# Slab weight sums of a Strassen-style down projection: the second row's sum made by an accumulating DMA, VectorE's two sums placed behind the second job

## The chip, the cores and the metric

The kernel runs on one core of one Trainium2 chip. A core has a matrix engine (TensorE, PE in the profile, with its weight loads listed apart as PEld), VectorE (DVE), ScalarE (ACT), GpSimd (POOL) and SyncE (SP), and 16 DMA engines that serve the queues of all of them. In this kernel SP issues the plain loads and POOL the loads that add to what is in place already (accumulating DMAs). The metric is the device time of one execution in microseconds.

## The reference

A two-layer decoder trunk in float32 on 256 tokens with width 2048. Each layer has a mixer and then a squared-ReLU MLP with 8192 hidden channels:

```python
def squared_relu_mlp(h, w1, w2):
    z = jax.nn.relu(h @ w1)
    return (z * z) @ w2
...
    x = x + jnp.concatenate([token_out, mem_out], axis=-1) @ w_out[i]
    x = x + squared_relu_mlp(rms_norm(x, ffn_norm[i]), w_ff1[i], w_ff2[i])
```

The mixers (causal pooling in the first layer, differential attention in the second, memory cross-attention in both) are not touched by the change. It concerns the product with `w_ff2` in both layers.

## The kernel before

All weights lie in DRAM as rows of 128 partitions x 1024 floats, in the order of their use. A weight that PE is to use is split in two: ScalarE casts it to PE's rounded format (the high part, line 178), and VectorE subtracts that from the weight (the low part, line 181). Both go to a ring of six slots of 512 columns. Each product is then three matmuls: low activations by high weights, high by high, and high by low (lines 867, 869, 870).

The feed (class `Feed`) does this ahead of PE. It holds a list of steps, `prep`, worked out by a dry run of the whole program (class `Plan`): N steps for 512 columns of an ordinary matrix, S steps for the jobs of a slab, and K steps for sums. When PE's program reaches a job, `fill` prepares up to six steps beyond it, as far as slots are free, and `load` issues DMAs up to three or four rows beyond what the step needs. SP issues ordinary rows (`raw`, line 135), a slab's first row (line 139), its second row (line 143) and the left half of a running sum (line 152).

Down projection by slabs. Most of `w_ff2` is multiplied by a scheme of the Strassen-Winograd kind: the 256 tokens are two halves, 256 rows of the weight are two blocks of 128, and 1024 columns are two halves of 512. A slab has four weight pieces: B11 and B21 in its first row in DRAM (`ra` in the code, left and right half), B12 and B22 in its second (`rb`). Instead of eight products it takes seven, on sums of pieces, in four jobs:

- job 0 uses B11 and B21, the untouched first row;
- job 1 uses the running sum `t1` = B11 + B12. It is made by DMA: SP loads B11, and POOL adds B12 to it with an accumulating DMA (line 153). There are three buffers for it, and it is fetched a slab ahead;
- job 2 uses the second row: in its left half t2 = t1 - B22, made by VectorE (line 204, the K step, ahead of job 0), and in its right half B22;
- job 3 uses the first row after VectorE has replaced it (line 218, 1024 columns, right behind the low part of job 0): t2 - B11 and t2 - B21.

The seven products are summed in seven PSUM banks (`banks`), two groups of columns by turns; sums of activations for them are made on VectorE (lines 792 to 795). At the end of each half the banks are put together with additions and subtractions (`close_left`, `finish_banks`). There are 60 slabs in each of the two layers. For even slabs both rows come from a pool of three buffers named `slab`; the second row of an odd slab lies in a fixed piece of the tile `room`, as do the running sums, so the profile names these `room`.

The order in which each engine gets its instructions is set by the framework's scheduler from the program's order and the dependences, and by a few hints (`order`) that put one instruction behind another. Up-projection tiles (`x_bank`, weights from `raw`) and slab jobs alternate by a table of due times (`tiles_at`). The program is symmetric in the two layers.

Of the kernel before, what the change touches and what calls it, by code (L numbers as in the profile page):

```python
# [17 lines left out]
P = 128  # L18
# [37 lines left out]
class Plan:  # L56
# [13 lines left out]
    def close(self):  # L70
        prep = []
        for job in self.jobs:

            if job[0] == "S" and job[2] == 0:
                prep.append(("K", job[1]))
            prep.append(job)
        self.prep = prep
        self.where = {job: i for i, job in enumerate(prep)}
        self.loads = []
        self.need = {}  # L80
        for p in prep:
            if p[0] == "K":
                self.loads += [("S", p[1], 0), ("S", p[1], 1)]
            elif p[0] == "N" and p[1] % 2 == 0:
                self.loads.append(("N", p[1] // 2))
            self.need[p] = len(self.loads) - 1
        rows = sorted(self.loads, key=lambda r: r[0] == "N" and 8 * r[1] + 8 > self.npos)
        self.row = {r: h for h, r in enumerate(rows)}
        of = {}
        pos = 0  # L90
        for what in self.entries:
            of.setdefault(pos // 8, []).append(what)
            pos += what[4]
        self.order = []
        for r in rows:
            self.order += of[r[1]] if r[0] == "N" else self.slabs[r[1]][r[2]]


class Feed:
# [22 lines left out]
    def load(self, upto):  # L122
        while self.lp < min(upto, len(self.plan.loads)):
            r = self.plan.loads[self.lp]
            h = self.plan.row[r]
            n = 1024
            if r[0] == "N":
                n = min(1024, (self.plan.npos - 8 * r[1]) * P)
                t = self.wpool.tile([P, 1024], F32, tag="raw", bufs=RAWS, name=f"raw{h}")
            elif r[2] and r[1] % 2:  # L130
                t = self.spare
            else:
                t = self.rows.tile([P, 1024], F32, tag="rows", bufs=3, name=f"slab{h}")
            if r[0] == "N":
                self.nc.sync.dma_start(t[:, 0:n], self.wst[h, :, 0:n])
            elif r[2] == 0:
                if r[1] % PER_PART == 0:
                    self.first_sum(r[1])
                self.nc.sync.dma_start(t, self.wst[h])
                if (r[1] + 1) % PER_PART:  # L140
                    self.first_sum(r[1] + 1)
            else:
                self.nc.sync.dma_start(t[:, 512:1024], self.wst[h, :, 512:1024])
            self.raw[r] = t
            self.lp += 1

# [41 lines left out]
        return True  # L188

    def _prepare(self, p):  # L190
        sub, add = self.nc.vector.tensor_sub, self.nc.vector.tensor_add
        self.load(self.plan.need[p] + 1 + self.loads_ahead)
        if p[0] == "N":
            r = ("N", p[1] // 2)
            c = p[1] % 2 * 512
            if not self._split(p, self.raw[r][:, c : c + 512], 1):
                return False
            if c:
                del self.raw[r]
            return True  # L200
        ra, rb = self.raw[("S", p[1], 0)], self.raw.get(("S", p[1], 1))
        t1 = self.t1[p[1] % len(self.t1)]
        if p[0] == "K":
            one = sub(rb[:, 0:512], t1, rb[:, 512:1024])
            if p[1] % PER_PART:
                self.order(one, self.last_low.ins.name)
            if self.gate:

                self.order(one, self.gate)
                self.gate = None  # L210
            return True
        src, n = ((ra, 2), (t1, 1), (rb, 2), (ra, 2))[p[2]]
        if not self._split(p, src, n):
            return False
        if p[2] == 0:
            t2 = rb[:, 0:512].unsqueeze(1).to_broadcast([P, 2, 512])
            two = ra.rearrange("p (a c) -> p a c", a=2)
            sub(two, t2, two)
        if p[2] == 1:
            self.t1_of[p[1] % len(self.t1)] = None  # L220
        if p[2] == 3:
            del self.raw[("S", p[1], 0)], self.raw[("S", p[1], 1)]
        return True

# [67 lines left out]
def program(ctx, tc, plan, dry, xT, memT, par, lam, cst, wst, yT):  # L292
# [437 lines left out]
    def ffn(l, xs, tags, done):  # L730
# [35 lines left out]
        def convert(j):  # L766
            a = stage[j % 8]
            k = j % NK

            def high():  # L770
                z_free[k] = False
                nc.scalar.copy(z[:, k, 0:T], a)
                at(1, low)

            def low():
                nc.vector.tensor_sub(z[:, k, T : 2 * T], a, z[:, k, 0:T].bitcast(F32))
                z_done.add(j)

            when(lambda: z_free[k], high)
            if j % 2 == 0:  # L780
                return
            i = j // 2

            def ready():
                return j in z_done and j - 1 in z_done and sit_free[i % 4]

            def combine():
                sit_free[i % 4] = False
                a11, a21 = stage[2 * i % 8][:, 0:P], stage[2 * i % 8][:, P:T]
                a12, a22 = stage[(2 * i + 1) % 8][:, 0:P], stage[(2 * i + 1) % 8][:, P:T]  # L790
                s1, s2, s3, s4 = (sums[i % 2][:, c * P : c * P + P] for c in range(4))
                nc.vector.tensor_add(s1, a21, a22)
                nc.vector.tensor_sub(s3, a11, a21)
                nc.vector.tensor_sub(s2, s1, a11)
                nc.vector.tensor_sub(s4, a12, s2)
                at(1, sums_high)
                at(2, sums_low)

            def sums_high():
                nc.scalar.copy(sit[i % 4][:, 0:512], sums[i % 2])  # L800

            def sums_low():
                nc.vector.tensor_sub(
                    sit[i % 4][:, 512:1024], sums[i % 2], sit[i % 4][:, 0:512].bitcast(F32)
                )
                sit_done.add(i)

            when(ready, combine)
# [63 lines left out]
        def slab_jobs(g, i, again, end):  # L872
            k = 2 * i
            first = 2 if g == 0 else 0
            n = feed.slab(
                [
                    [("w_ff2", l, k, c, 4), ("w_ff2", l, k + 1, c, 4)]
                    for c in (first, first + 1)
                ]
            )  # L880

            def plain(c, t):
                assert k + c in z_done
                zk = z[:, (k + c) % NK, :]
                return zk[:, t * P : t * P + P], zk[:, T + t * P : T + t * P + P]

            def summed(c):
                assert i in sit_done
                s = sit[i % 4]
                return s[:, c * P : c * P + P], s[:, 512 + c * P : 512 + c * P + P]  # L890

            sides = (
                ((0, lambda: plain(0, 0)), (1, lambda: plain(1, 0))),
                ((2, lambda: summed(0)),),
                ((3, lambda: summed(1)), (4, lambda: summed(3))),
                ((5, lambda: summed(2)), (6, lambda: plain(1, 1))),
            )

            def run(j):
                hi, lo = feed.job(n, j)  # L900
                for c, (p, a) in enumerate(sides[j]):
                    s = slice(512 * c, 512 * c + 512)
                    assert holds[p] == g
                    product(p, g, end, a(), hi[:, s], lo[:, s])
                feed.job_used(n, j)
                if j == 3 and not again:
                    sit_free[i % 4] = True
                    if i < 24:
                        z_free[k % NK] = z_free[(k + 1) % NK] = True

            return run
# [6 lines left out]
        holds = [0] * 7  # L918
        back = [False] * 7
        saved = {}  # L920
        of_job = ((0, 1), (2,), (3, 4), (5, 6))

        def restore(p, g):
            if (g, p) in saved:
# [16 lines left out]
        def close_left(j):  # L941
# [8 lines left out]
                nc.scalar.copy(left["v"], banks[2])  # L950
            elif j == 2:
                left["c12"] = keep.pop(0)
                add(left["u"], left["u"], banks[3])
                sub(left["c12"], left["v"], left["u"])
                add(left["c12"], left["c12"], banks[4])
            else:
                u, v = left["u"], left["v"]
                add(u, u, banks[5])
                sub(v, v, u)
                sub(u, u, banks[6])  # L960
            for p in of_job[j]:
                restore(p, 0)
            if j == 3:
# [27 lines left out]
        def finish_banks():  # L991
# [9 lines left out]
            add(c11, u, p2)  # L1001
            add(u, u, p6)
            sub(c12, v, u)
            add(u, u, p7)
            add(c12, c12, p3)
            sub(v, v, u)
            sub(u, u, p4)
            for c, t in ((c11, 0), (c12, 0), (u, 1), (v, 1)):
                scale_rows(c, t)

# [627 lines left out]
```

## Time and profile before

| what | value |
|---|---|
| median of 3 runs | 2010.63 us (2010.59 to 2010.78) |
| span of the profiled execution | 2010.7 us |
| PE busy | 1999.0 us (99%) |
| VectorE busy | 1779.2 us (88%) |
| ScalarE busy | 1525.3 us (76%) |
| POOL busy | 157.1 us (8%) |
| moved by DMA | 422.19 MB, 210 GB/s |
| accumulating DMAs | 120, each 256 KB |

The profiled execution's span is the kernel's time to within 0.1 us, with nothing around it. Busy times of matmuls are modelled at their ends, so a busy PE can still hide short waits; these stand in the view of waits. A DMA share is the time of packets over 16 engines, and can exceed 1 where packets wait on each other. L178 and the like are line numbers of the kernel before.

### The profile page before, as it was taken

The page shows a single profiled execution, that of the slowest core. Times are in us where ns is not written, and L with a number is a line of the kernel's source. Part 1 is how long each engine was busy: PE and PEld are TensorE (multiplying, and loading weights), DVE is VectorE, ACT ScalarE, POOL GpSimd, SP SyncE. Part 2 cuts the span into 40 slices and gives each one's busy share as a digit, 9 for nine tenths or more (in the row PEclk, how much of TensorE's full clock was granted, in tenths as well). Part 3 has the DMA queues.
Part 4 walks back from the last instruction along what each step waited for, and adds up shares of the span by engine and source line. Part 5 has one row for each costly group of instructions (what it writes and reads, how often), then busy time and mean ns, then how long its engine had stood idle before and what let it go on. Part 6 is the DMA issues. An engine that isn't in the chain of part 4 may idle for free.

```text
span 2010.7 us, 31966 instructions
## 1 busy us (share of the span) xinstructions
PE 1999.0 (99%) x10510; PEld 1696.5 (84%) x10510; DVE 1779.2 (88%) x3096; ACT 1525.3 (76%) x2838; POOL 157.1 (8%) x187
## 2 busy tenths in 40 slices
PE   9999999999999999999999999999999999999999
PEld 8888888888888888888888888888888888888877
DVE  8888888989999999999765698878989999999998
ACT  7765577787887888878665699557787878878885
POOL 0001310000000000100000000320000000100000
PEclk9999999999999999999999999999999999999999
DMA  8555576777778777755575533567777777777773
GB/s 319 171 188 195 188 221 208 232 221 229 226 226 240 223 218 234 225 175 175 181 235 194 178 127 126 199 197 229 224 214 233 225 234 223 231 230 231 223 228 124
DMA packets 145030, 422.19 MB, mean 210 GB/s; under 512 B 16352, under 2 KB 19040, under 8 KB 144864
## 3 DMA queue, kind: packets, MB, share of 16 engines
q1 hardware_dynamic: 127440, 388.69, 57.5%
q0 software_dynamic: 17280, 31.46, 9.7%
q8 instruction: 82, 1.34, 0.3%
q14 instruction: 84, 0.69, 0.1%
q10 hardware_dynamic: 144, 0.01, 0.0%
HBM read 418.00 MB, written 2.10 MB: 209 GB/s over the span
## 4 chain that ended last, share of the span: by engine, by line
PE 93%; ACT 3%; DVE 2%; issue 1%; DMA 0%; ACTq 0%; DVEq 0%
PE x_bank L433 21%; PE x_bank L435 11%; PE p L867 9%; PE p L870 9%; PE p L869 9%; PE wo L433 6%; PE wo L435 3%; PE u L433 2%; ACT hi_ring L178 1%; PE ff L433 1%; PE u L435 1%; PE k L469 1%; PE q L467 1%; PE q L469 1%; PE q L468 1%; PE v L468 1%
## 5 line engine op out<-in xcount | busy, mean ns | idle before, releaser
L178 ACT CAST hi_ring<-raw 128x512 fp32r<-128x512 f32 x969 | 593.5, 623 | 267.3 <-PE x_bank L433 61.1
L181 DVE TENSOR_TENSOR lo_ring<-raw,hi_ring 128x512 fp32r<-128x512 f32 x969 | 662.0, 695 | 105.1 <-ACT hi_ring L178 93.5
L433 PE MATMUL x_bank<-fx,hi_ring 128*128 128x512 f32 x1952 | 610.8, 394 | 0.0
L435 PEld LDWEIGHTS x_bank<-fx,lo_ring 128*128 128x128 f32 x1952 | 365.1, 188 | 88.1 <-DVE lo_ring L181 6.1
L181 DVE TENSOR_TENSOR lo_ring<-slab,hi_ring 128x1024 fp32r<-128x1024 f32 x300 | 366.4, 1221 | 50.1 <-ACT hi_ring L178 48.8
L178 ACT CAST hi_ring<-slab 128x1024 fp32r<-128x1024 f32 x300 | 314.6, 1053 | 117.2 <-PE p L869 65.0
L435 PE MATMUL x_bank<-fx,lo_ring 128*128 128x256 f32 x1952 | 384.8, 278 | 1.5 <-DVE lo_ring L181 1.5
L433 PEld LDWEIGHTS x_bank<-fx,hi_ring 128*128 128x128 f32 x1952 | 320.7, 189 | 26.8 <-ACT room L761 1.3
L153 POOL DMA_DIRECT2D room<-in_w x120 | 104.0, 872 | 1139.7 <-DMA room<-in_w 1121.4
L867 PE MATMUL p<-hi_ring,sit 128*128 128x512 f32 x480 | 190.5, 397 | 0.4 <-ACT hi_ring L178 0.2
L869 PE MATMUL p<-hi_ring,sit 128*128 128x512 f32 x480 | 187.9, 391 | 0.0
L870 PE MATMUL p<-lo_ring,sit 128*128 128x512 f32 x480 | 186.5, 391 | 0.2
L433 PE MATMUL wo<-cat,hi_ring 128*128 128x512 f32 x512 | 161.8, 397 | 0.3 <-DVE rc L404 0.3
L181 DVE TENSOR_TENSOR lo_ring<-room,hi_ring 128x512 fp32r<-128x512 f32 x180 | 154.3, 863 | 5.7 <-ACT hi_ring L178 5.6
L178 ACT CAST hi_ring<-room 128x512 fp32r<-128x512 f32 x180 | 138.1, 769 | 19.0 <-PE p L869 9.5
L867 PE MATMUL p<-hi_ring,z 128*128 128x512 f32 x360 | 141.2, 392 | 0.7 <-ACT hi_ring L178 0.7
L869 PE MATMUL p<-hi_ring,z 128*128 128x512 f32 x360 | 140.6, 391 | 0.0
L870 PE MATMUL p<-lo_ring,z 128*128 128x512 f32 x360 | 139.7, 392 | 0.0
L435 PEld LDWEIGHTS wo<-cat,lo_ring 128*128 128x128 f32 x512 | 95.9, 188 | 22.0
L870 PEld LDWEIGHTS p<-lo_ring,sit 128*128 128x128 f32 x480 | 89.8, 188 | 21.8 <-DVE lo_ring L181 2.7
L867 PEld LDWEIGHTS p<-hi_ring,sit 128*128 128x128 f32 x480 | 90.0, 187 | 15.6 <-ACT hi_ring L178 5.8
L435 PE MATMUL wo<-cat,lo_ring 128*128 128x256 f32 x512 | 101.5, 279 | 0.0
(370 smaller groups left out, 3339.9 us busy)
## 6 DMA issues: line engine op xcount, KB each, us to landing
raw<-in_w SPq DMA_DIRECT2D x484, 512.0 KB, 4.3
slab<-in_w SPq DMA_DIRECT2D x120, 512.0 KB, 4.4
room<-in_w SPq DMA_DIRECT2D x180, 256.0 KB, 3.3
room<-in_w POOLq DMA_DIRECT2D x120, 256.0 KB, 5.7
slab<-in_w SPq DMA_DIRECT2D x60, 256.0 KB, 4.3
memraw<-in_mem SPq DMA_DIRECT2D x5, 512.0 KB, 4.5
resid<-in_x SPq DMA_DIRECT2D x8, 256.0 KB, 5.5
out_y<-resid SPq DMA_DIRECT2D x16, 128.0 KB, 1.9
```

Of the source, the lines that this page charges most:

```text
L153: self.nc.gpsimd.dma_start(self.t1[i], right, accum_op=ALU.add)
L178: self.last_cast = self.nc.scalar.copy(hi, src)
L181: low = self.nc.vector.tensor_sub(lo, src, hi.bitcast(F32))
L433: nc.tensor.matmul(ps, hi, xs[:, k, :], start=first and c == 0, stop=False)
L435: nc.tensor.matmul(ps[:, T : 2 * T], lo, xs[:, k, 0:T], start=False, stop=last and c == len(ks) - 1,)
L467: nc.tensor.matmul(ps[t], x[t][1], hi, start=k == 0, stop=False)
L468: nc.tensor.matmul(ps[t], x[t][0], hi, start=False, stop=False)
L469: nc.tensor.matmul(ps[t], x[t][0], lo, start=False, stop=k == NK - 1)
L867: nc.tensor.matmul(ps, a[1], hi, start=new, stop=False, **again)
L869: nc.tensor.matmul(ps, a[0], hi, start=False, stop=False, **again)
L870: nc.tensor.matmul(ps, a[0], lo, start=False, stop=end, **again)
```

## The change

- The second row is loaded whole, 512 KB instead of its right half of 256 KB, and POOL then adds B22 to its left half with a second accumulating DMA. That half becomes B12 + B22, where it was t2 = B11 + B12 - B22.
- VectorE's two sums per slab become plain additions of 512 columns on the first row: its left half becomes t1 + B22, and its right half that plus B21. The sum of 1024 columns goes.
- These two stand in the K step, which moves from ahead of job 0 to behind job 1, and a hint puts the first of them behind the low part of job 1.
- The scheme of seven products is another one of the same family. So signs change in the sums of activations and in the closing of the banks, and the products with sums 1 and 2 change places: job 2 now holds banks 5 and 4, and job 3 banks 3 and 6.

```diff
@@ class Plan, close
-            if job[0] == "S" and job[2] == 0:
+            prep.append(job)
+            if job[0] == "S" and job[2] == 1:
                 prep.append(("K", job[1]))
-            prep.append(job)
...
-            if p[0] == "K":
+            if p[0] == "S" and p[2] == 0:
                 self.loads += [("S", p[1], 0), ("S", p[1], 1)]
@@ class Feed, load
-                self.nc.sync.dma_start(t[:, 512:1024], self.wst[h, :, 512:1024])
+                self.nc.sync.dma_start(t, self.wst[h])
+                self.nc.gpsimd.dma_start(t[:, 0:512], self.wst[h, :, 512:1024], accum_op=ALU.add)
@@ class Feed, _prepare
         if p[0] == "K":
-            one = sub(rb[:, 0:512], t1, rb[:, 512:1024])
-            if p[1] % PER_PART:
-                self.order(one, self.last_low.ins.name)
+            one = add(ra[:, 0:512], t1, rb[:, 512:1024])
+            self.order(one, self.last_low.ins.name)
+            add(ra[:, 512:1024], ra[:, 0:512], ra[:, 512:1024])
...
-        if p[2] == 0:
-            t2 = rb[:, 0:512].unsqueeze(1).to_broadcast([P, 2, 512])
-            two = ra.rearrange("p (a c) -> p a c", a=2)
-            sub(two, t2, two)
-        if p[2] == 1:
+        if p[2] == 3:
             self.t1_of[p[1] % len(self.t1)] = None
-        if p[2] == 3:
@@ ffn, combine
-                nc.vector.tensor_add(s1, a21, a22)
-                nc.vector.tensor_sub(s3, a11, a21)
+                nc.vector.tensor_sub(s1, a21, a22)
+                nc.vector.tensor_sub(s3, a21, a11)
                 nc.vector.tensor_sub(s2, s1, a11)
-                nc.vector.tensor_sub(s4, a12, s2)
+                nc.vector.tensor_add(s4, a12, s2)
@@ ffn, slab_jobs
-                ((3, lambda: summed(1)), (4, lambda: summed(3))),
-                ((5, lambda: summed(2)), (6, lambda: plain(1, 1))),
+                ((5, lambda: summed(2)), (4, lambda: summed(3))),
+                ((3, lambda: summed(1)), (6, lambda: plain(1, 1))),
...
-        of_job = ((0, 1), (2,), (3, 4), (5, 6))
+        of_job = ((0, 1), (2,), (5, 4), (3, 6))
@@ ffn, close_left
-                add(left["u"], left["u"], banks[3])
-                sub(left["c12"], left["v"], left["u"])
-                add(left["c12"], left["c12"], banks[4])
+                add(left["c12"], left["v"], banks[4])
+                sub(left["c12"], left["c12"], left["u"])
+                sub(left["u"], left["u"], banks[5])
...
-                add(u, u, banks[5])
+                sub(left["c12"], left["c12"], banks[3])
+                add(u, u, banks[3])
                 sub(v, v, u)
-                sub(u, u, banks[6])
+                add(u, u, banks[6])
@@ ffn, finish_banks
-            add(u, u, p7)
+            sub(u, u, p7)
...
-            sub(u, u, p4)
+            add(u, u, p4)
```

More of the change, by code (lines that the diff above doesn't have):

```diff
@@ L190, in _prepare @@
     def _prepare(self, p):
-        sub, add = self.nc.vector.tensor_sub, self.nc.vector.tensor_add
+        add = self.nc.vector.tensor_add
         self.load(self.plan.need[p] + 1 + self.loads_ahead)
```

## The prediction

> **What bounds the kernel now.** I read the page's busy table and chain first, to find the engine that sets the end.
>
> ```profile
> PE 1999.0 (99%) x10510; PEld 1696.5 (84%) x10510; DVE 1779.2 (88%) x3096; ACT 1525.3 (76%) x2838; POOL 157.1 (8%) x187
> PE 93%; ACT 3%; DVE 2%; issue 1%; DMA 0%; ACTq 0%; DVEq 0%
> ```
>
> PE is busy 1999.0 of 2010.7 us and makes up 93% of the chain; VectorE is second. The change does not touch the number of matmuls, so it can only win what PE waits for, and can lose as much as late weights cost. Slabs exist only in the two squared-ReLU layers, so I then cut those into stages, with two dense moments beside them.
>
> ```profile
> core 0: us, PE busy (x) PEld busy (x) DVE busy (x) ACT busy (x) POOL busy (x), PEclk, DMA share, GB/s
> 10.00:15.00 5.00, 5.00 (x24) 4.14 (x23) 4.72 (x15) 5.00 (x12) 0.00 (x0) 1.00 1.03 410
> 400.00:600.00 200.00, 199.70 (x1019) 168.66 (x1018) 184.43 (x275) 163.33 (x281) 16.44 (x19) 1.00 0.74 225
> 600.00:800.00 200.00, 199.83 (x1018) 168.78 (x1017) 188.31 (x281) 167.28 (x281) 17.30 (x20) 1.00 0.77 230
> 1400.00:1600.00 200.00, 199.55 (x1022) 168.88 (x1022) 182.42 (x273) 160.06 (x273) 16.42 (x19) 1.00 0.74 224
> 1600.00:1800.00 200.00, 199.99 (x1018) 169.17 (x1017) 190.01 (x284) 162.45 (x271) 16.67 (x20) 1.00 0.76 229
> 1589.00:1594.00 5.00, 5.00 (x27) 4.26 (x26) 5.00 (x7) 4.71 (x10) 0.86 (x1) 1.00 1.04 346
> ```
>
> In the slab stages VectorE is busy 92 to 95%, and the DMA engines show a share of 0.74 to 0.77. The POOL column counts the accumulating DMAs: 19 or 20 in 200 us, so one slab takes about 10.3 us. The waits of PE and of its weight loads then say what a lighter VectorE can give back.
>
> ```profile
> PEld x_bank L435 <- DVE lo_ring L181: 7.8, 21, 1.0
> PEld p L867 <- ACT hi_ring L178: 7.3, 23, 0.5
> PEld p L870 <- DVE lo_ring L181: 5.3, 18, 0.5
> PE x_bank L435 <- DVE lo_ring L181: 2.0, 5, 0.6
> ```
>
> Columns: waiter, releaser, us in total, times, longest. VectorE ends 7.8 + 5.3 + 2.0 = 15.1 us of waits. That is the ceiling of the gain; weight loads run beside matmuls, so the part seen in the time is smaller.
>
> **Term 1, VectorE.** Per slab one 512-wide and one 1024-wide sum go, and two 512-wide additions come.
>
> ```profile
> L204 DVE TENSOR_TENSOR slab<-room,slab 128x512 f32<-128x512 f32 x60 | 41.1, 685 | 10.6 <-DMA room<-in_w 10.6
> L218 DVE TENSOR_TENSOR slab<-slab,slab 128x1024 f32<-128x1024 f32 x60 | 73.1, 1218 | 0.0
> ```
>
> Each has a twin of 60 for the other slabs. Saved per slab: 0.685 + 1.218 - 2 x 0.685 = 0.53 us, times 120 = 64 us of VectorE, 5% of a 10.3 us slab, so its share there falls from about 93 to 88%. Swapping additions and subtractions in the activations' sums and in the bank sums has the same shapes and costs nothing; the closing of the left half has one 512-wide operation more, 0.7 us per layer, on an engine that then has over 10% free. Gain on the path: between 0 (PE's waits stay, since other casts set them) and 15.1 us. I take a quarter, 3.8 us: of the rows above, the weight-load ones are partly hidden, and the waits at the layers' ends have other causes too.
>
> The 10.6 us in the first row are VectorE's waits for the first slab's running sum, once per layer; the new place of the sums, behind job 1, which needs that sum anyhow, makes them disappear from VectorE. I count no time for it: PE is fed from slots filled earlier.
>
> Where the two sums now stand, seen on VectorE for one odd slab in the first layer (slab_4509 before, slab_4526 after, is its first row; room holds its second row and the running sum). Before:
>
> ```order
> L204 TENSOR_TENSOR room_2604<-room_2604 128x512
> L181 TENSOR_TENSOR lo_ring<-slab_4509,hi_ring 128x1024
> L181 TENSOR_TENSOR lo_ring<-room_2604,hi_ring 128x512
> L218 TENSOR_TENSOR slab_4509<-room_2604,slab_4509 128x1024
> L181 TENSOR_TENSOR lo_ring<-raw_4499,hi_ring 128x512
> ```
>
> and after:
>
> ```order
> L182 TENSOR_TENSOR lo_ring<-slab_4526,hi_ring 128x1024
> L182 TENSOR_TENSOR lo_ring<-room_2604,hi_ring 128x512
> L205 TENSOR_TENSOR slab_4526<-room_2604 128x512
> L182 TENSOR_TENSOR lo_ring<-raw_4516,hi_ring 128x512
> L207 TENSOR_TENSOR slab_4526<-slab_4526 128x512
> ```
>
> The first sum moved behind the low parts of jobs 0 and 1, and the second is half as wide.
>
> **Term 2, the second accumulating DMA.** It stands in POOL's queue, which runs in order. Before, POOL held only the running sums between the squares of two layers:
>
> ```order
> L706 TENSOR_TENSOR psq<-resid 128x256
> L707 TENSOR_TENSOR acc<-acc,psq 128x256
> L153 DMA room_2604<-in_w 128x512 x60
> L700 TENSOR_TENSOR acc<-resid 128x256
> L706 TENSOR_TENSOR psq<-resid 128x256
> ```
>
> and after, at the start of that run:
>
> ```order
> L154 DMA room_2604<-in_w 128x512 x3
> L144 DMA room_2604<-in_w 128x512
> L154 DMA room_2604<-in_w 128x512
> L144 DMA slab_3025<-in_w 128x512
> L154 DMA room_2604<-in_w 128x512
> ```
>
> Running sums (L154) and second-row sums (L144) alternate. The first operand of job 2 thus changes from a VectorE product to: load landed, then POOL issues, then the sum landed. Durations, and one of the tighter (even) slabs from load to use:
>
> ```profile
> L143 SPq DMA_DIRECT2D slab<-in_w x60: 327/328/328, 104.8 to 1959.0; - x60
> DMA to landing us min/median/max: 2.5/4.0/6.9
> L153 POOL DMA_DIRECT2D room<-in_w x120: 856/865/1226, 257.7 to 1954.3; - x120
> DMA to landing us min/median/max: 3.6/5.7/8.0
> 613.23 0.33 SPq L143 DMA_DIRECT2D slab<-in_w  x1
> 617.31 0.33 SPq L152 DMA_DIRECT2D room<-in_w  x1
> 619.38 0.33 SPq L143 DMA_DIRECT2D room<-in_w  x1
> 621.29 0.86 POOL L153 DMA_DIRECT2D room<-in_w  x1 [8.94 <-DMA room<-in_w]
> 626.09 1.05 ACT L178 CAST hi_ring<-slab 128x1024 fp32r<-128x1024 f32 x1
> 628.05 1.22 DVE L181 TENSOR_TENSOR lo_ring<-slab,hi_ring 128x1024 fp32r<-128x1024 f32 x1
> 630.90 1.05 ACT L178 CAST hi_ring<-slab 128x1024 fp32r<-128x1024 f32 x1 [0.84 <-PE x_bank L433]
> 630.93 0.40 PE L867 MATMUL p<-hi_ring,sit 128*128 128x512 f32 x1
> 636.39 1.05 ACT L178 CAST hi_ring<-room 128x1024 fp32r<-128x1024 f32 x1 [0.59 <-PE p L869]
> 644.99 0.62 ACT L178 CAST hi_ring<-room 128x512 fp32r<-128x512 f32 x1
> ```
>
> The second row is issued at 613.23 and job 2's cast starts at 626.09. The load lands after 4.0 us, the sum 5.7 us after POOL starts it: 613.23 + 4.0 + 0.1 + 5.7 = 623.0, so 3.1 us early. The low part ends at 629.27 and PE first uses the job at 630.93, which adds 1.7 us: the chain may grow by 4.8 us before PE feels it. The next, odd slab has more: its second row, issued at 619.38, is cast at 636.39, 17.0 us later instead of 12.9. Job 3, which reads VectorE's two sums, is cast only at 630.90, so their new place does not hold it up. POOL has the time: 2 x 0.87 us per 10.3 us. A running sum that queues behind a second-row sum loses at most some 4 us; the one loaded at 617.31 is cast two slabs later, at 644.99. SP issues as many DMAs as before; its running-sum load (L152) now waits for the moved sum too, about 1 us later, and delays what is queued behind it. That is the loads of the other weights, for which ScalarE hardly ever waits:
>
> ```profile
> ACT hi_ring L178 <- DMA raw<-in_w: 6.3, 4, 2.4
> ```
>
> so I count nothing; without that cover it would be up to 1 us per slab.
>
> **Term 3, DMA traffic.** Per slab the load grows by 256 KB (the left half) and the sum reads 256 KB more: 0.524 MB per 10.3 us, 51 GB/s. Two readings of what that means:
>
> ```profile
> q1 hardware_dynamic: 127440, 388.69, 57.5%
> q0 software_dynamic: 17280, 31.46, 9.7%
> slab<-in_w SPq DMA_DIRECT2D x120, 512.0 KB, 4.4
> ```
>
> By packets' time: q0 doubles (9.7% of 2010.7 = 195 us) and q1 grows by 31.46 MB x 1156 us / 388.69 MB = 94 us; 289 us over 120 slabs is 2.4 us per 10.3 us, a share of 0.23 on top of 0.74 to 0.77, so 0.97 to 1.00. By bytes: 225 to 230 GB/s become about 280, while the stage at 1589 to 1594, with running sums in the mix, moved 346 at a share of 1.04, so 333 at 1.00; that is 84%. Packets' time contains waiting for one another (the share exceeds 1 in both dense rows), so bytes are nearer to capacity, and I take 84%: the DMA engines are close to full but not the bound. The larger load costs little in landing: 512 KB landed in 4.4 us against 4.0 us. Price of late sums: 0 at least; at most the rivals below. I take 1.4 us, some five even slabs late by 0.3 us.
>
> The Trainium skill (DMA: Bandwidth & Descriptors, Latency and other measured facts) puts HBM access at 0.2 us on average and 2 us at high load. By that rule each of the two landings could grow by 1.8 us, an estimate from the page, and the sum would still hold since 3.6 us is under 4.8. The trace agrees in kind, with medians 1.5 and 2.1 us above the minima at a share of 0.75; it is why the second rival below is not given less.
>
> **Sum.** 2010.7 (the profiled span; the median of the runs, 2010.63, is the same) - 3.8 + 1.4 = 2008.3 us. About 0.2%, 4 us, is what I take as telling a change from none; so this is no change.
>
> **Rivals.**
> 1. VectorE's relief is worth more: half of the 15.1 us or more goes, and no sum is late: 2010.7 - 7.5 = 2003.2. For it: VectorE at 95% in the later stages. Against: 7.3 us of waits are ended by ScalarE, which has as much work as before.
> 2. Slower: the two landings of the second-row sum lengthen under the added traffic. Place: job 2's cast, with ScalarE's queue held behind it. It decides when both together grow by more than 4.8 us on even slabs; an average of 0.3 us late on 60 slabs is 18 us: 2010.7 - 2.4 + 18 = 2026. For it: landings already reach 6.9 and 8.0 us, 5.2 us above the medians together. Against: those are the extremes.
> 3. Slower: the DMA engines run out. If packets' time is the true measure and the second sums stretch other packets, the demand passes 1.00; 2% over, on 120 slabs of 10.3 us, is 25 us: 2036, with all weight loads late and not only the sums. It decides at a capacity below 280 GB/s for this mix.
>
> **Chances.** The forecast 0.45 (its own range 2006.7 to 2014.6), rival 1 0.20, rival 2 0.23, rival 3 0.12. So faster 0.20, same 0.45, slower 0.35. The range goes from 2002, under rival 1, to 2036, which leaves out the upper half of rival 3 and a little of each of the others.
>
> **What the new profile would show.** VectorE's busy time near 1715 us; the 1024-wide sum gone and 240 additions of 512 near 0.685 us. POOL with 240 accumulating DMAs at about 0.87 us. DMA share in the slab stages 0.9 to 1.0 and about 280 GB/s. If I am right, ScalarE waits for the second-row DMA in few slabs and landings stay under 5.5 and 7 us. A wait of ScalarE at job 2's cast for a DMA, in tens of times, would show rival 2; weight casts of the other matrices waiting for their loads too, rival 3; PE's waits for VectorE under half of 15.1 us without either, rival 1.

## The result and the profile after

The changed kernel takes 2018.79 us (median of 16 runs, 2013.31 to 2023.51), the kernel before in the same runs 2010.73 us (16 runs, 2009.26 to 2013.72). The ratio is 1.0036 with a 95% interval of 1.0028 to 1.0044: some 7 to 8 us slower, where no change had been forecast. The profiled execution of the changed kernel took 2020.91 us and has a span of 2019.1 us. A span does leave some time out, 1.7 to 2.2 us in every run here that has both figures. So the profile of the kernel before, with a span of 2010.7 us, is not within 0.1 us of its execution's time: by that difference it belongs to an execution of some 2012.5 us. The prediction's sum still starts from the right time, the median of the runs.

Busy times of the engines, the chain of waits by engine, and the two main DMA queues (packets, MB, share of 16 engines) of the changed kernel:

```profile
PE 1996.9 (99%) x10510; PEld 1697.4 (84%) x10510; DVE 1725.7 (85%) x3098; ACT 1519.9 (75%) x2838; POOL 260.8 (13%) x307
q1 hardware_dynamic: 127440, 420.14, 61.3%
q0 software_dynamic: 34560, 62.93, 18.3%
PE 90%; ACT 4%; DVE 3%; issue 1%; DMA 1%; DVEq 0%; ACTq 0%; SPq 0%
```

VectorE got its relief (1779.2 to 1725.7 us), and PE does the same work, yet ScalarE, VectorE and DMA hold more of the chain. The four slab stages of the changed kernel:

```profile
400.00:600.00 200.00, 196.79 (x996) 165.91 (x995) 170.99 (x270) 161.03 (x274) 32.01 (x37) 0.99 0.92 269
600.00:800.00 200.00, 198.19 (x1002) 166.06 (x1001) 175.77 (x276) 162.72 (x277) 33.71 (x39) 1.00 0.95 279
1400.00:1600.00 200.00, 199.59 (x1024) 169.23 (x1023) 173.76 (x273) 160.65 (x276) 31.13 (x36) 1.00 0.93 270
1600.00:1800.00 200.00, 197.72 (x1005) 166.74 (x1004) 178.29 (x282) 157.10 (x266) 34.22 (x40) 1.00 0.95 277
```

PE does 996 to 1005 matmuls in three of the four stages, where before it did 1018 or 1019. (A PE that is "busy" 199.59 of 200 us says less than the count, since the ends of matmuls are modelled.) The waits of PE and of its weight loads (PEld) at the slab products (`p`) and the up-projection tiles (`x_bank`):

```profile
PE p L863 <- ACT hi_ring L179: 6.8, 12, 2.0
PE x_bank L431 <- DVE lo_ring L182: 3.9, 6, 1.6
PE p L866 <- DVE lo_ring L182: 2.5, 6, 0.6
PEld p L863 <- ACT hi_ring L179: 12.1, 22, 2.4
PEld x_bank L431 <- DVE lo_ring L182: 7.6, 9, 2.0
PEld p L866 <- DVE lo_ring L182: 7.6, 14, 1.0
```

The row of the kernel before that answers to the first of these:

```profile
PE p L867 <- ACT hi_ring L178: 0.9, 5, 0.2
```

The new waits stand at `p`, the slab products: 6.8 us of PE where it was 0.9, and the longest wait of a weight load is almost five times as long as before (2.4 us against 0.5). Slab weights come late from ScalarE, and then from VectorE. The view of waits does not say why ScalarE is late. For the one late slab below, it names PE (line 866) as what released the cast, and POOL's ten idle microseconds are put down to VectorE. The instructions themselves, slab 22 of the first layer (counted from 0), changed kernel:

```profile
510.11 0.33 SPq L143 DMA_DIRECT2D slab<-in_w  x1
519.55 0.86 POOL L144 DMA_DIRECT2D slab<-in_w  x1 [10.00 <-DVE lo_ring L182]
527.85 1.04 ACT L179 CAST hi_ring<-slab 128x1024 fp32r<-128x1024 f32 x1 [3.97 <-PE p L866]
528.95 0.50 PE L863 MATMUL p<-hi_ring,sit 128*128 128x512 f32 x1 [2.02 <-ACT hi_ring L179]
530.21 0.80 PE L866 MATMUL p<-lo_ring,sit 128*128 128x512 f32 x1 [0.53 <-DVE lo_ring L182]
```

The load is issued at 510.11 and takes 8.8 us, to 518.9; POOL starts the sum 0.6 us later, at 519.55; the sum takes 8.2 us, to 527.8; and the cast of job 2 starts at 527.85, after 3.97 us in which ScalarE had nothing else to do. PE waits 2.02 us. The cast starts 0.07 us behind the sum's landing, so it was the sum that it waited for, whatever releaser the view names: a wait for several semaphores is put down to one of them.

The wait has an aftermath. From 529.7 us on, for 3.4 us, the granted clock of PE is 0.50, and PE starts a matmul every 0.43 us where it had started one every 0.23:

```profile
529.90:533.20 3.30, 2.99 (x8) 2.41 (x9) 3.30 (x6) 1.99 (x4) 0.86 (x1) 0.51 0.70 223
```

By estimate that is some 1.5 us of PE's work lost on top of the waits (the 2.9 us from 530.2, where PE's second wait ends, at half the clock).

The trace's records give the landings and the start of job 2's cast for every slab. The six even slabs with the longest idle time of ScalarE before that cast, and what the two kinds of slab show (microseconds; the first two slabs of each layer are left out):

```
slab   load     load    sum      sum     cast     ScalarE
       issued   landed  issued   landed  starts   idle before
22      510.11   518.93  519.55   527.78   527.85  3.97
30      596.08   603.58  604.20   611.21   611.37  3.69
46      760.08   767.39  768.01   775.20   775.26  1.92
82     1594.85  1602.32 1603.61  1611.62  1611.69  3.07
90     1678.64  1686.29 1686.91  1692.12  1692.28  2.03
114    1925.41  1930.35 1930.91  1938.61  1938.76  1.79

                                  even slabs      odd slabs
load landing, median (95%)        5.53 (7.64)     5.33 (7.17)
load landed to sum issued         0.56            0.53
sum landing, median (95%)         6.58 (8.21)     7.00 (9.07)
load issued to cast, median       15.23           18.13
sum landed to cast, min/25%/50%   0.07/0.24/1.50  2.39/4.04/4.98
```

On 14 of the even slabs job 2's cast starts within 0.16 us of the sum's landing, and ScalarE stood idle for 24.2 us before these 14 casts. On no odd slab does it come nearer than 2.39 us. The landings over all slabs in the changed kernel, of the second row's load (line 143; before 2.5/4.0/6.9 us):

```profile
DMA to landing us min/median/max: 3.3/5.4/8.8
```

and of the second-row sum (line 144; the running sum of before had 3.6/5.7/8.0 us):

```profile
DMA to landing us min/median/max: 3.7/6.9/9.9
```

This gave three theories. A: the second-row sum lands too late for job 2's cast on even slabs, and the casts behind it come late too. B: the sums as such cost it, by their traffic or in POOL's queue, whatever they are for. C: VectorE's two sums in their new place, or the larger loads, cost it.

### The profile page after: what moved, and what is told of

It reads as the page before. It is cut to its first block, busy times and chain, and to the rows that moved or that the text cites. A ratio compares the mean times of both kernels' runs of the same rounds, so it can differ in the third digit from the quotient of the medians.

```text
span 2019.1 us, 32409 instructions
## 1 busy us (share of the span) xinstructions
PE 1996.9 (99%) x10510; PEld 1697.4 (84%) x10510; DVE 1725.7 (85%) x3098; ACT 1519.9 (75%) x2838; POOL 260.8 (13%) x307
## 4 chain that ended last, share of the span: by engine, by line
PE 90%; ACT 4%; DVE 3%; issue 1%; DMA 1%; DVEq 0%; ACTq 0%; SPq 0%
PE x_bank L429 20%; PE x_bank L431 10%; PE p L863 9%; PE p L865 8%; PE p L866 8%; PE wo L429 6%; PE wo L431 3%; PE u L429 2%; ACT hi_ring L179 2%; DVE lo_ring L182 2%; PE ff L429 1%; PE u L431 1%; PE q L463 1%; PE q L465 1%; PE q L464 1%
## 5 line engine op out<-in xcount | busy, mean ns | idle before, releaser
L179 ACT CAST hi_ring<-room 128x512 fp32r<-128x512 f32 x180 | 138.1, 767 | 24.2 <-PE p L865 14.8
L144 POOL DMA_DIRECT2D slab<-in_w x60 | 51.9, 866 | 798.3 <-DVE osb L1493 352.9
```

What stands on the lines that cost most here:

```text
L144: self.nc.gpsimd.dma_start(t[:, 0:512], self.wst[h, :, 512:1024], accum_op=ALU.add)
L179: self.last_cast = self.nc.scalar.copy(hi, src)
```

## The experiments

All are edits of the changed kernel. A ratio is to the kernel before, run beside it on the same chip.

### e1: no second-row sum

```diff
-                self.nc.gpsimd.dma_start(t[:, 0:512], self.wst[h, :, 512:1024], accum_op=ALU.add)
```

> The changed kernel without its second accumulating DMA: job 2's left operand stays the plain left half of the second row, so the sum B12 + B22 is left out of the computation. Everything else, the whole second row's load and VectorE's two additions among it, stays. Theory A (the sum lands late for job 2's cast on even slabs, ScalarE stands and PE runs dry): the time falls to 2008 to 2011 us and PE's waits for casts fall back to about 15 us. Theory B (the DMA engines are too full, and all weight loads come late): it falls too, to about 2010, as the DMA share falls from 0.95 to about 0.8. Theory C (the new place and order of VectorE's sums, or the new order of products, costs the time): it stays at 2016 to 2019 us.

Measured: 2008.82 us (2008.36 to 2010.19), ratio 0.9992 (0.9983 to 1.0000). The loss is gone, with VectorE's sums in the new place and the larger loads kept: C is out for the changed kernel. Waits of PE and its weight loads in this kernel:

```profile
PE x_bank L430 <- DVE lo_ring L181: 3.9, 6, 1.6
PE p L862 <- ACT hi_ring L178: 1.9, 8, 0.3
PEld x_bank L430 <- DVE lo_ring L181: 7.1, 8, 2.0
PEld p L862 <- ACT hi_ring L178: 5.9, 20, 0.5
PEld p L865 <- DVE lo_ring L181: 1.1, 4, 0.4
```

The waits at `p` have shrunk, those at `x_bank` hardly moved: they have nothing to do with the sum. This run also measures the change without its price: with VectorE's relief and without the sum it is 0.08% faster, 1.6 us, between 0 and 3.4.

### e2: the sums aimed at a buffer that nobody reads

```diff
-                self.nc.gpsimd.dma_start(t[:, 0:512], self.wst[h, :, 512:1024], accum_op=ALU.add)
+                self.nc.gpsimd.dma_start(self.aside, self.wst[h, :, 512:1024], accum_op=ALU.add)
...
+        feed.aside = keep.pop()
+        nc.vector.memset(feed.aside, 0.0)
```

(The closing of the left half then has one spare bank less, and restores one bank earlier.)

> The changed kernel with the second accumulating DMA aimed at a buffer that nothing reads, so its traffic and its place in GpSimd's queue stay and job 2 waits for its load alone; the sum B12 + B22 is left out of job 2's operand. (The buffer is one of the nine for parked banks; the closing of the left half then restores one bank earlier.) Theory A: 2008 to 2012 us at a DMA share of about 0.95 in the slab stages. Theory B: 2016 to 2020 us, as the changed kernel. Theory C: 2016 to 2019 us.

Measured: 2261.21 us (2257.73 to 2266.84), ratio 1.125. None of the theories expected that, and it tells nothing of them. The waits of POOL and PE:

```profile
POOL keep L144 <- DMA keep<-in_w: 454.5, 115, 7.5
...
PEld st_x L488 <- POOL acc L703: 194.0, 2, 131.9
```

With nothing to wait for but their own buffer, the scheduler put the sums far ahead in POOL's queue, in front of the squares of the norm, and each waited for the one before it to land. PE stood twice at the norm, up to 131.9 us. The design was bad: an operation moved off its dependences is also moved in its queue. The question of the traffic went to e4.

### e3: the second-row sum made by VectorE

```diff
-                self.nc.gpsimd.dma_start(t[:, 0:512], self.wst[h, :, 512:1024], accum_op=ALU.add)
...
             self.order(one, self.last_low.ins.name)
+            add(rb[:, 0:512], rb[:, 0:512], rb[:, 512:1024])
```

> The changed kernel with the second-row sum made by VectorE in place (one more addition of 512 columns per slab) and not by DMA. VectorE then has 3 x 0.685 us per slab against 1.90 us before the change. Theory A: 2009 to 2012 us, about the kernel before. Theory B: the same. Theory C: 2016 us or more, since the places of the sums and the products' order stay and VectorE is as full as before.

Measured: 2021.28 us (2018.08 to 2023.84), ratio 1.0053 (1.0040 to 1.0065). Only theory C had forecast a time as long as this; since e1 excludes C for the changed kernel, this version must be slow for a reason of its own. VectorE is busy 1787.0 us, 0.4% more than before (1779.2), so the amount of its work alone is unlikely to be it. Waits in this kernel:

```profile
DVE room L206 <- DMA room<-in_w: 17.9, 14, 3.2
PEld p L866 <- DVE lo_ring L181: 9.7, 9, 3.2
ACT hi_ring L178 <- DVE slab L206: 9.2, 6, 1.8
PE p L866 <- DVE lo_ring L181: 6.1, 8, 2.8
```

Line 206 is the added sum. The hint binds only the first sum; this one the scheduler had put earlier (it starts 6.7 us ahead of the first in the median), where VectorE waits for the second row's load in front of other work in its queue. e7 and e8 below follow that up.

### e4: on even slabs the second row is fetched first

```diff
-                self.loads += [("S", p[1], 0), ("S", p[1], 1)]
+                c = (0, 1) if p[1] % 2 else (1, 0)
+                self.loads += [("S", p[1], c[0]), ("S", p[1], c[1])]
```

Both rows of an even slab take buffers of the same pool, so the second row now takes the buffer that comes free first. Every sum stays, with the same bytes.

> The changed kernel with the two rows of even slabs loaded in the other order, the second row first, so that it takes the buffer that comes free at the end of job 2 of two slabs before, and not that of job 3; its sum should land 3 to 4 us earlier, and the first row's load be issued as much later. Theory A: 2007 to 2011 us, with few waits at job 2's cast, unless the first row now comes late for job 0. Theory B: 2016 to 2020 us, since the traffic is the same. Theory C: 2016 to 2019 us.

Measured: 2009.27 us (2008.72 to 2012.71), ratio 0.9995 (0.9986 to 1.0004). The loss is gone with all the traffic in place. The first and the last of its slab stages:

```profile
400.00:600.00 200.00, 199.34 (x1017) 168.81 (x1016) 175.31 (x276) 164.35 (x281) 32.82 (x38) 1.00 0.96 275
...
1600.00:1800.00 200.00, 199.68 (x1020) 169.42 (x1019) 180.24 (x284) 160.09 (x269) 34.29 (x40) 1.00 0.98 282
```

The landings of the second row's load, and of its sum, in e4:

```profile
DMA to landing us min/median/max: 3.3/5.3/7.9
```

```profile
DMA to landing us min/median/max: 4.9/7.1/9.4
```

The DMA share is higher than in the changed kernel (0.96 and 0.98 against 0.92 and 0.95) and the landings are as slow. What differs is the start: from issue to job 2's cast an even slab has a median of 17.9 us instead of 15.23, and the sum lands 4.98 us ahead of the cast in the median (5% below 2.04 us, one slab at 0.16). The first row pays for it, with a median of 10.6 us from issue to job 0's cast instead of 13.6, but it still lands at least 0.83 us ahead on every even slab. Slab 22 in this kernel:

```profile
506.32 0.33 SPq L144 DMA_DIRECT2D slab<-in_w  x1
...
510.73 0.86 POOL L145 DMA_DIRECT2D slab<-in_w  x1 [1.19 <-DVE room L816]
...
523.88 1.05 ACT L180 CAST hi_ring<-slab 128x1024 fp32r<-128x1024 f32 x1
```

Its second row is issued 3.8 us earlier, and PE's waits at `p` are those of e1 again:

```profile
PE p L864 <- ACT hi_ring L180: 1.9, 8, 0.3
PEld p L864 <- ACT hi_ring L180: 6.1, 20, 0.5
PEld p L867 <- DVE lo_ring L183: 1.2, 4, 0.4
```

B is out as the cause of the loss: the sums' traffic, and POOL's part in them, cost nothing that these runs can tell from zero as long as each sum starts in time. The version removes the loss, but it cannot be told from the kernel before.

### e5 and e6: the sum on even slabs only, and on odd slabs only

```diff
-                self.nc.gpsimd.dma_start(t[:, 0:512], self.wst[h, :, 512:1024], accum_op=ALU.add)
+                if r[1] % 2 == 0:
+                    self.nc.gpsimd.dma_start(t[:, 0:512], self.wst[h, :, 512:1024], accum_op=ALU.add)
```

e6 has `if r[1] % 2:` in its place. Both move the same bytes.

> The changed kernel with the second row's accumulating sum made only on even slabs; on odd slabs it is left out, so that B12 + B22 is missing there and job 2 uses B12 alone. Half of the sums' traffic remains, on exactly the slabs where the trace of the changed kernel showed casts that waited for it. Theory A (late sums on even slabs): most of the loss stays, though the landings shorten with the smaller traffic, so 2010 to 2017 us, with casts of job 2 starting within 0.2 us of the sum's landing on several even slabs and on no odd one. Theory B (the sums' traffic or POOL's queue as such): half of the loss, near 2013 us, and the same in the next run. Theory C (VectorE's three additions behind job 1): 2009 us, as without any sum.

> The changed kernel with the second row's accumulating sum made only on odd slabs; on even slabs it is left out, so that B12 + B22 is missing there. The same number of sums and the same bytes as in the run with even slabs alone, but only where there is slack. Theory A: no sum is late, and the time is that without any sum, 2008 to 2009.5 us. Theory B: the same time as with the even slabs alone, near 2013 us.

Measured: e5 2015.04 us (2012.99 to 2019.47), ratio 1.0022 (1.0013 to 1.0031); e6 2009.11 us (2008.73 to 2010.97), ratio 0.9992 (0.9983 to 1.0001). The first slab stage in e5, then in e6:

```profile
400.00:600.00 200.00, 198.81 (x1014) 167.81 (x1013) 174.61 (x274) 164.12 (x281) 25.12 (x30) 1.00 0.88 263
```

```profile
400.00:600.00 200.00, 199.12 (x1014) 168.29 (x1013) 174.65 (x275) 163.97 (x280) 24.18 (x28) 1.00 0.88 264
```

The waits at `p` for ScalarE in e5, then in e6:

```profile
PEld p L864 <- ACT hi_ring L180: 9.0, 21, 2.2
...
PE p L864 <- ACT hi_ring L180: 4.4, 10, 1.7
```

```profile
PEld p L864 <- ACT hi_ring L180: 6.2, 21, 0.5
...
PE p L864 <- ACT hi_ring L180: 1.9, 8, 0.3
```

Equal traffic (share 0.88, 263 and 264 GB/s), and 6 us between them: the even slabs carry the loss, the odd ones none. That is theory A, and the landings say the same: in e5 job 2's cast starts within 0.16 us of the sum's landing on 11 of the even slabs, and in e6 on no odd slab nearer than 2.73 us. The loss in e5 is smaller than in the changed kernel; its sums land sooner (median 6.0 us, against 6.58 on the even slabs there), and before the 11 casts ScalarE stood idle for 11.1 us, not 24.2. (The expectation speaks of three additions of VectorE; e5 has the two of the changed kernel.)

### e7 and e8: VectorE's sum spread out, and held back

e7 is e3 with the last of VectorE's three additions moved behind job 2:

```diff
-            add(ra[:, 512:1024], ra[:, 0:512], ra[:, 512:1024])
...
+        if p[2] == 2:
+            add(ra[:, 512:1024], ra[:, 0:512], ra[:, 512:1024])
```

> The second row's sum made in place by VectorE on every slab, as in the earlier run at 2021 us (output as the reference's), but the last of the three additions, which only job 3 needs, moved from behind job 1 to behind job 2. VectorE's work is the same to the instruction, about 1787 us. If the burst of three additions between two low parts made that run slow, PE's waits for low parts fall from 9.7 + 6.1 us to under 6 us together and the time to 2011 to 2014 us. If VectorE's amount of work made it slow, it stays at 2018 to 2023 us.

e8 is e3 with the added sum bound behind the first:

```diff
-            add(rb[:, 0:512], rb[:, 0:512], rb[:, 512:1024])
+            own = add(rb[:, 0:512], rb[:, 0:512], rb[:, 512:1024])
+            self.order(own, one.ins.name)
```

> VectorE's sum of the second row in place, as in the run at 2021 us, but the order of VectorE's work pins it behind the first sum instead of letting it stand some 4 us earlier, where the trace of that run shows VectorE waiting 17.9 + 3.9 us for the second row's load (18 waits). VectorE's work stays at 1787 us. If those waits in VectorE's queue made that run slow, they go, and with them most of PE's 9.7 + 6.1 us of waits for low parts: 2010 to 2013 us. If the amount or the spacing of VectorE's work made it slow, PE's waits and the time stay, 2017 to 2024 us, with VectorE's waits for loads gone.

Measured: e7 2024.60 us (2020.81 to 2027.20), ratio 1.0065 (1.0052 to 1.0078); e8 2028.45 us (2026.59 to 2029.75), ratio 1.0083 (1.0069 to 1.0096). A burst of three additions was not it: with them spread, PE's waits for low parts rose from 9.7 + 6.1 us to 12.5 + 6.7, and the trace of e3 had not shown the three in a row either. In e8 VectorE's waits for the load are gone, as expected, and so are most of PE's for low parts. But the time rose, beyond both ranges of the expectation:

```profile
PEld p L864 <- ACT hi_ring L178: 24.5, 34, 2.9
ACT hi_ring L178 <- DVE slab L206: 18.6, 14, 2.0
PE p L864 <- ACT hi_ring L178: 12.8, 20, 2.5
ACT hi_ring L178 <- DVE room L206: 7.0, 9, 1.1
```

Now ScalarE waits 25.6 us, in 23 waits, for the sum itself, and PE for ScalarE. It is the same spot as in the changed kernel, job 2's first operand finished only when it should be cast already, with VectorE in the place of the DMA. In e3 and e7 the loss is divided between that wait and VectorE's waits for loads; how much each has, and what share the spacing or the amount of VectorE's work has, stays open.

## Why the prediction was wrong

**What failed: Term 2's step from medians to a margin, "613.23 + 4.0 + 0.1 + 5.7 = 623.0, so 3.1 us early", "the chain may grow by 4.8 us".** Three things in it were off.

- The landings were taken from a profile at a share of 0.74 to 0.77 and left at that, though Term 3 forecast 0.97 to 1.00. "The larger load costs little in landing: 512 KB landed in 4.4 us against 4.0" was read at the old traffic too. Under the new one the load took 5.4 us and the sum 6.9 (5.53 and 6.58 on even slabs): 2.4 us of the 4.8 gone in the median.
- POOL starts a sum 0.56 us after the landing, not 0.1: another 0.5 us. No row shows the 0.1, and the trace of before had the same delay for its running sums already, 0.53 us in the median.
- What then remained, some 2 us, is less than the scatter. In slab 22 the load took 3.3 us and the sum 1.6 us more than those medians. The prediction knew that the extremes lay 5.2 us above the medians and set it aside as "those are the extremes"; but with 60 tight slabs, the slowest tenth is six of them, and a cast that is late holds up the casts behind it in ScalarE's queue.

The budget itself was right: 12.9 us from issue to cast in the slab that was quoted, and 12.44 us at the 5% mark of the even slabs afterwards. Odd slabs were rightly called safe.

**Term 3, "1.4 us, some five even slabs late by 0.3 us", was mis-sized as a result.** It measured some 9 us, give or take 2.4 (ratio 1.0036 less e1's 0.9992), with 14 even slabs released by the sum and, over these, 1.7 us of idle ScalarE each (0.3 at the same casts in e1). What happened is rival 2, at its place and by its mechanism, given 0.23. Its price of 18 us was twice too high, but not in the lateness: before job 2's casts on even slabs ScalarE stood idle for 39.7 us, in e1 for 19.5, and the 20.2 us between them are 0.35 us per even slab, about the 0.3 that the rival had taken. The rival passed all of it on to the time. The span of the profiled execution is 12.3 us longer than e1's, so part of the lateness did not reach PE; what did came with a price that the prediction did not have, the half clock behind slab 22's wait. (Rival 2's 2.4 us are the forecast's 3.8 - 1.4, so the 1.4 us of late sums are in it twice.) The sign to look for, "a wait of ScalarE at job 2's cast for a DMA, in tens of times", was badly chosen: the view of waits of the changed kernel puts only 3 waits of ScalarE, 1.8 us, down to the sum, and only start times set against landings show them.

**Term 1, 3.8 us, was of the right kind and somewhat large.** Without the sum the gain was 1.6 us (0 to 3.4). VectorE's 15.1 us of waits became 12.1 (7.1 + 3.9 + 1.1, in e1): of the rows at `p` 5.3 us became 1.1, but those at `x_bank` rose from 9.8 to 11.0. Most of the ceiling belonged to waits at `x_bank`, which stayed; the prediction had allowed for waits of that kind. (VectorE's share in the slab stages of before was 91 to 95% by the rows shown, not 92 to 95.) VectorE's busy time came near the forecast (1725.7 for 1715), POOL's count and the price of its instructions as forecast.

**The traffic was read rightly.** 269 to 279 GB/s at a share of 0.92 to 0.95 was close to the forecast 280 and 0.97 to 1.00, and e4 moved 282 GB/s at 0.98 without a loss: nearly full by packets' time, but not the bound. Rival 3 is excluded by that, and by the other weights' casts, which wait for their loads hardly longer than the 6.3 us of before; the row in the changed kernel:

```profile
ACT hi_ring L179 <- DMA raw<-in_w: 6.8, 6, 2.4
```

**The Trainium skill's rule** (DMA: Bandwidth & Descriptors, Latency and other measured facts) gave each landing up to 1.8 us more at high load, by an estimate from the page. The medians grew by 1.4 and 1.2 us, within that bound, so the trace agrees in size and the rule was nearer than the sum, which used none of it; whether the growth is access to HBM or waiting in the DMA queues, no run here shows. The mistake was to call 3.6 under 4.8 safe: it left 1.2 us for a scatter that was known to be larger.

## What to carry to other kernels

When an operand is moved from an engine to a chain of DMAs, add up the chain at the traffic that the change will make and with the slow landings, not the median ones, and count how many tiles have less margin than that. If some have, look first at what lets the chain begin: here the same transfers in another order of loads (e4) cost nothing. And to see who held an instruction that waits for several things, set its start against the landings rather than trust the one releaser that a view names.

## What the runs showed of the hardware

- Landings rise well before the DMA engines bind. The second row's 512 KB took 4.6 us in e1 (share 0.81 to 0.84), 5.0 in e5 (0.87 to 0.91) and 5.4 in the changed kernel (0.92 to 0.95), all with the same loads in the same order; in e4, with another order, 5.3 (0.95 to 0.98). The row of e1:

```profile
DMA to landing us min/median/max: 3.2/4.6/8.8
```

- The versions with late sums scatter more from run to run: the changed kernel's 16 runs span 10.2 us and e5's 11 runs 6.5, while the 11 runs each of e1, e4 and e6 span 1.8, 4.0 and 2.2. Scatter alone is no sign of a late DMA, though: e7, where VectorE makes the sum, spans 6.4 us in five runs.
- The granted clock falls to half where PE stands still, and takes some microseconds to come back. In e2 PE stood still from 256.9 to 388.6 us; three stretches of that wait and of the time behind it:

```profile
300.00:388.00 88.00, 0.00 (x0) 0.00 (x0) 0.00 (x0) 0.00 (x0) 33.90 (x45) 0.50 0.40 63
388.60:392.00 3.40, 3.38 (x10) 2.81 (x11) 0.32 (x1) 1.90 (x5) 2.68 (x3) 0.50 0.64 109
395.00:400.00 5.00, 5.00 (x32) 4.38 (x31) 3.49 (x10) 3.50 (x9) 0.00 (x0) 1.00 0.67 225
```

- A wait of some 2 us can be followed by such a fall too. At the slab products, 3.4 us at half clock follow PE's wait of 2.02 us in the changed kernel, of 2.75 in e3 and one of two, 2.52 and 2.51 us long, in e8. That gives no limit: none follow a wait of 1.84 us in e7, and between the two layers of the kernel before they follow two shorter waits close together, 1.2 and 0.7 us, which in e1 are followed by none.
